# A two-layer hybrid trunk on one core: first loads, GLA state sums, RWKV state products, attention transposes and the last norm rearranged

## The chip, the core and the metric

The kernel runs on one core of one Trainium2 chip. The metric is the device time of one execution in microseconds; all times below are microseconds unless ns is said. TensorE (PE) multiplies matrices out of SBUF into PSUM, VectorE (DVE), ScalarE (ACT) and GpSimd (POOL) work on vectors, and SyncE (SP) issues most DMAs. Each of them runs its own instructions in a fixed order, so an instruction that waits holds up all that is behind it on its engine.

## What is computed

`x` is 512 tokens of 1024 features, in fp32. Each of two layers mixes tokens, attends to a memory of 256 tokens and applies a gated feed-forward net; a norm ends the trunk. The first layer's mixer is GLA beside RWKV-7, the second's is RG-LRU beside mLSTM. Cut to what the change touches:

```python
mem_n = rms_norm(mem, mem_norm_g)
h = x
for layer in range(2):
    xn = rms_norm(h, norm_mix_g[layer])
    proj = xn @ w_in
    if layer == 0:                               # y_b: mLSTM in layer 1
        y_a, y_b = gla_group(proj[..., :GLA_COLS]), rwkv7_group(proj[..., GLA_COLS:])
    h = h + concat([y_a, y_b]) @ w_mix_out[layer]
    h = h + memory_cross_attention(rms_norm(h, g), mem_n)  # 4 heads of 256, softmax over 256
    h = h + conv_glu_ffn(rms_norm(h, g))
return rms_norm(h, final_norm_g)

# gla_chunked: 8 chunks of 64 tokens, 4 heads
scores = where(causal, q_dec @ k_inv.T, 0);  o_local = scores @ v
o_state = q_c @ S;  S = S * sd_c + ke_c.T @ v_c

# rwkv7_chunked: 8 heads of 64
z_state, z_local = triangular_solve(I - A_ab, [a_dec, A_ak @ v])
z = zs @ S.T + zl                                # one step a chunk
y = rd @ S.T + arb @ z + yl
S = S * sd + z.T @ be + v_c.T @ ke_c
```

## The kernel before

Features lie on the 128 partitions, tokens along the free axis, so an activation is eight tiles of 128x512 (four for a half). Each fp32 factor is split into two fp32r parts, and a product is three matmuls (hi·hi, hi·lo, lo·hi). `wload` brings in a weight tile of 128x1024 (512 KB): a DMA on SP's queue into `raw` (ring `wr`, three buffers), a copy to `wh` on ACT, and a subtraction to `wl` on DVE, which frees the `raw` buffer. `dense` then issues 24 matmuls of 128x512 that sum into one PSUM tile of the pool `mm` (three buffers); these are the "dense matmuls" below, mm<-xs,wh and mm<-xs,wl in the profile. Small products go to the PSUM pool `ax` (five buffers). `qr` is a ring of sixteen 128x512 tiles named `xs`. The function `mmul` is line 209, `act` line 206, `tt` 194, `stt` 203, so most rows name these lines and are told apart by tiles.

What order the instructions of each engine take is settled when the program is built: a scheduler takes the program's operations with their dependences and places one list on each engine. `issue_after` makes an operation wait in that list for a given instruction. Nothing is reordered when the program runs.

**Head.** Set-up loads vectors (`vec`) and constants (`cmat`: identity, a block matrix `bo64`, the mask `rmask`), runs warm-up matmuls on a constant tile, and scales `bo64` to `bo64m` on DVE. `trunk` then loads x's first tile, a small weight (`walr`, made on ACT and DVE from its own load), the GLA key weights `wk`, and x's other seven tiles.

**GLA** (line 593): after the projections, scores are masked into `sc` by copies on DVE; `kt` and `v` give the state sums (28 products for two head pairs and seven chunks), `S` is updated by chunk on DVE, and both feed the outputs.

**RWKV** (line 767) treats p = 0..3, two heads each. Per p: three dense blocks r, k, v (72 dense matmuls), `wa,w2a` products for decay and gate, a chain of exponentials on ACT (`e1`, `a`), a scan on DVE (`e2`, line 814), norm of k (`kn,cmat`), the stacks `stk`, `bk`, products `stk,bk` masked into `bb` and `stk`, transposes into SV and BKT, and a bonus product `xs,cmat`. After p=0 `during` calls `memory_norm` (line 484): it loads the memory in four tiles, squares them on ACT and adds them into `nacc` on DVE; the rest of it runs after p=2. Then comes a triangular solve, mostly on DVE, beside the memory's key projections, and the chunk loop: eight chunks, each with products stk,sv (w), sv,stk (yp), ws,bb (z), sv,bkt (uu) and bb,sv (yp), eight of each kind, with the memory's projections as dense matmuls of 128x256 among them.

**Attention** (`heads`, line 427): per head and half, scores, softmax parts `mx`, `e`, `sm`, then four transposes of `e` into `pT`. **End** (`finish`, line 1336): for each half of the tokens, the last add to h, the norm's sum, and eight products h * gain * r with four stores.

Of the kernel before, what the change touches and what calls it, by code (L numbers as in the profile page):

```python
# [20 lines left out]
KD = 8  # L21
# [121 lines left out]
class Trunk:  # L143
    def __init__(self, ctx, tc, I):
# [14 lines left out]
        nc.gpsimd.dma_start(out=self.cm, in_=I["cmat"][:, 0:384])  # L159
# [10 lines left out]
        for i in range(10):  # L170
            self.mmul(warm[:, 0:P], self.ones["d"], self.ones["d"])
# [6 lines left out]
        nc.vector.tensor_scalar(out=self.bo64m, in0=self.bo64, scalar1=1.0 / 64.0, scalar2=None, op0=ALU.mult)  # L178
# [61 lines left out]
    def wload(self, src, kb, m):  # L240
# [4 lines left out]
        n = kb * m  # L245
        self.last_load = nc.sync.dma_start(out=raw[:, :n], in_=src.rearrange("p k m -> p (k m)"))
        self.act(hi[:, :n], raw[:, :n], AF.Copy)
        self.tt(lo[:, :n], raw[:, :n], hi[:, :n].bitcast(F32), ALU.subtract)
        sh = lambda t: t[:, :n].rearrange("p (k m) -> p k m", m=m)
# [149 lines left out]
def xattn(K, l, nm, kd, vd, h, feed):  # L399
    nc, X = K.nc, nm.X  # L400
    with ExitStack() as es:
# [25 lines left out]
        def heads(hd, q):  # L427
            pT = [K.ax.tile([P, T], F32, name="ax") for _ in range(2)]
            for half in range(2):
# [18 lines left out]
                for i in range(2):  # L448
# [3 lines left out]
                    for m in range(2):  # L452
                        nc.tensor.transpose(pT[m][:, t * P:(t + 1) * P], e[:, i, m * P:(m + 1) * P], K.ident)  # L453
# [30 lines left out]
def memory_norm(K, sm):  # L484
# [5 lines left out]
    for i in range(4):  # L490
# [3 lines left out]
        sq = K.qr.tile([P, T], F32, name="xs") if i else acc  # L494
# [7 lines left out]
    r = K.qr.tile([P, T], F32, name="xs")[:, 0:256]  # L502
# [90 lines left out]
def gla(K, nm, wga, wk, squares, after, Y):  # L593
    nc, X = K.nc, nm.X
    with ExitStack() as es:
# [5 lines left out]
        with K.tc.issue_after(after.ins):  # L601
            nc.vector.tensor_copy(out=gm, in_=gf)
        wa = gp.tile([48, 256], F32, name="walpha")
# [96 lines left out]
        for p in range(2):  # L700
            us = {}
            for c in range(7):
                if c % 4 < 2:
                    us[c // 4, c % 2] = K.ax.tile([P, 2, P], F32, name="ax")
                u = us[c // 4, c % 2][:, (c % 4) // 2]
                r = slice(64 * (c % 2), 64 * (c % 2) + 64)
                for e in range(2):
                    hd = 2 * p + e
                    K.mmul(u[64 * e:64 * e + 64], kt[p][r, c // 2, 64 * e:64 * e + 64],
                           v[r, c // 2, hd * P:(hd + 1) * P])  # L710
                if c == 0:
# [55 lines left out]
def rwkv(K, X, Y, during, after):  # L767
# [3 lines left out]
    with ExitStack() as core:  # L771
# [12 lines left out]
        with ExitStack() as es:  # L784
# [13 lines left out]
            vp = wt.tile([P, 640], F32, name="vp")  # L798
            nc.gpsimd.memset(vp, 0.0)
            for p in range(4):  # L800
                r = shifted(K, new(), K.block("w_rw", p, X), p, om)
                k = shifted(K, new(), K.block("w_rw", 4 + p, X), 4 + p, om)
                v = shifted(K, vp[:, 64:576], K.block("w_rw", 8 + p, X), 8 + p, om)
# [28 lines left out]
                for w0, w1 in ((0, 4), (4, 8), (8, 9)):  # L832
                    ps = K.ax.tile([P, 4, P], F32, name="ax")
                    for w in range(w0, w1):
                        nc.tensor.transpose(ps[:, w - w0], vp[:, w * 64:w * 64 + P], K.ident)
# [532 lines left out]
```

## Time and profile before

| | us |
|---|---|
| median of 3 runs | 1558.81 (1558.35 to 1563.36) |
| profiled execution | 1558.83 |
| its span | 1557.0 |
| PE busy | 1527.6 |
| DVE busy | 914.9 |
| ACT busy | 683.7 |
| POOL busy | 23.3 |

The span runs from the first to the last instruction of the profiled execution; 1.8 lie around it. The page gives shares for the whole span, so a stage has to be read from the rows of its own stretch. A matmul is pipelined: its mean in a list of groups is its latency, and what it costs in a stream is the spacing, best seen in the chain of waits, which gives the time of a whole run of them. The mean granted clock of PE is 0.996 of 2.4 GHz; a few stretches lie under that.

### The profile page before, as it was taken

Reading aid. Unit: us, or ns where it says so; the run is one execution under the profiler, and the core shown is the slowest. Engines: PE = TensorE matmul, PEld = TensorE weight load, DVE = VectorE, ACT = ScalarE, POOL = GpSimd, SP = SyncE. Lnnn points to the kernel's source line nnn. Section 1 sums busy time; section 2 is a strip of 40 time slices with the busy share of each in tenths; the row PEclk is TensorE's granted clock in tenths of the full one; section 3 lists DMA queues with packets and bytes.
Section 4 is the critical chain, followed back from the end, with each engine's and each line's share of the span. In section 5 each row is a group of like instructions: output and inputs, shape, how many; then the busy total and the mean of one; then the engine's idle time right before and its main releaser. Section 6 shows DMA issues by size and latency. Waiting matters only on the chain.

```text
span 1557.0 us, 20187 instructions
## 1 busy us (share of the span) xinstructions
PE 1527.6 (98%) x8077; PEld 1240.3 (80%) x8077; DVE 914.9 (59%) x1348; ACT 683.7 (44%) x1101; POOL 23.3 (1%) x62
## 2 busy tenths in 40 slices
PE   8999999999999999999999999999999999999997
PEld 6876777787888888888888878788888888888886
DVE  7537679645655755556633386777557556565333
ACT  5465563345444543333332267566345333333221
POOL 2000000001000000000000000000000000000000
PEclk9999999999999999999999999999999999999999
DMA  4222226226331333332233321224213333322332
GB/s 165 81 75 82 68 62 192 90 93 224 111 106 48 107 97 98 99 95 95 92 98 102 94 98 49 75 73 149 72 51 117 105 98 95 96 95 89 101 98 78
DMA packets 50175, 152.19 MB, mean 98 GB/s; under 512 B 5505, under 2 KB 8865, under 8 KB 50081
## 3 DMA queue, kind: packets, MB, share of 16 engines
q1 hardware_dynamic: 45664, 142.87, 29.2%
q10 hardware_dynamic: 3536, 5.38, 1.0%
q0 software_dynamic: 880, 2.66, 0.4%
q8 instruction: 63, 1.03, 0.3%
q14 instruction: 32, 0.25, 0.1%
HBM read 144.59 MB, written 6.29 MB: 97 GB/s over the span
## 4 chain that ended last, share of the span: by engine, by line
PE 89%; DVE 6%; ACT 3%; DMA 1%; issue 1%; SPq 0%; DVEq 0%; ACTq 0%
PE mm L209 77%; PE ax L209 10%; DVE wl L194 1%; ACT e L206 1%; PE ax L453 1%; ACT wh L206 1%; DVE tm L194 1%; DVE bb L892 0%; DVE tu L194 0%; DMA raw<-in_w_kv 0%; DMA raw<-in_w_gla 0%; DVE au L881 0%; DVE e L814 0%; ACT a L206 0%; DVE stk L203 0%
## 5 line engine op out<-in xcount | busy, mean ns | idle before, releaser
L209 PE MATMUL mm<-xs,wh 128*128 128x512 f32 (+1 forms) x3627 | 1110.4, 387 | 2.4 <-DVE vp L203 1.8
L209 PEld LDWEIGHTS mm<-xs,wh 128*128 128x128 f32 x3627 | 671.8, 188 | 147.9 <-issue 8.0
L209 PE MATMUL mm<-xs,wl 128*128 128x512 f32 (+1 forms) x1814 | 700.3, 386 | 0.6 <-DVE wl L194 0.5
L206 ACT ACTIVATE wh<-raw 128x1024 fp32r<-128x1024 f32 (+2 forms) x273 | 264.8, 970 | 528.5 <-PE mm L209 412.1
L194 DVE TENSOR_TENSOR wl<-raw,wh 128x1024 fp32r<-128x1024 f32 (+2 forms) x272 | 302.6, 1113 | 211.8 <-ACT wh L206 210.8
L209 PEld LDWEIGHTS mm<-xs,wl 128*128 128x128 f32 x1814 | 341.0, 188 | 71.9 <-issue 1.8
L194 DVE TENSOR_TENSOR upad<-mm,rstd 128x512 f32<-128x512 f32 (+1 forms) x52 | 35.9, 690 | 95.5 <-PE mm L209 95.3
L194 DVE TENSOR_TENSOR h<-h,mm 128x512 f32<-128x512 f32 (+1 forms) x73 | 49.5, 677 | 69.3 <-PE mm L209 69.1
L194 DVE TENSOR_TENSOR g<-mm,rstd 128x512 f32<-128x512 f32 (+1 forms) x44 | 30.4, 692 | 76.0 <-PE mm L209 75.9
L203 DVE SCALAR_TENSOR_TENSOR c<-upad,vec,c 128x512 f32<-128x512 f32 (+1 forms) x88 | 65.9, 749 | 3.3 <-ACT c L206 1.8
L209 PE MATMUL mm<-wh,xs 128*128 128x256 f32 (+1 forms) x256 | 66.4, 349 | 0.0
L206 ACT ACTIVATE c<-c 128x512 f32<-128x512 f32 (+1 forms) x44 | 27.8, 632 | 87.1 <-DVE c L203 87.1
L209 PEld LDWEIGHTS mm<-wh,xs 128*128 128x128 f32 x256 | 44.8, 194 | 6.3 <-issue 1.0
L209 PE MATMUL mm<-wl,xs 128*128 128x256 f32 (+1 forms) x128 | 45.3, 354 | 3.8 <-DVE wl L194 3.8
L206 ACT ACTIVATE xs<-g 128x512 fp32r<-128x512 f32 (+1 forms) x44 | 27.8, 633 | 26.9 <-DVE g L194 26.9
L206 ACT ACTIVATE c<-upad,vec 128x512 f32<-128x512 f32 (+1 forms) x44 | 35.3, 802 | 1.5 <-DVE upad L194 1.5
L206 ACT ACTIVATE e<-ax,mx,scl 128x256 f32<-128x256 f32 x32 | 17.8, 560 | 39.8 <-DVE mx L194 39.8
L194 DVE TENSOR_TENSOR g<-c,g 128x512 f32<-128x512 f32 (+1 forms) x44 | 30.4, 692 | 5.8 <-ACT c L206 1.4
L194 DVE TENSOR_TENSOR nacc<-nacc,nsq 128x512 f32<-128x512 f32 x45 | 32.8, 730 | 0.3
L203 DVE SCALAR_TENSOR_TENSOR xs<-h,vec,xs 128x512 fp32r<-128x512 f32 x40 | 29.9, 749 | 3.5 <-ACT xs L206 3.4
L194 DVE TENSOR_TENSOR xs<-ax,xs 128x512 fp32r<-128x512 f32 x32 | 21.3, 687 | 18.0 <-ACT xs L206 18.0
L206 ACT ACTIVATE xs<-h,vec 128x512 fp32r<-128x512 f32 x40 | 28.8, 719 | 6.5 <-DVE h L194 6.5
(353 smaller groups left out, 1221.9 us busy)
## 6 DMA issues: line engine op xcount, KB each, us to landing
raw<-in_w_up SPq DMA_DIRECT2D x86, 512.0 KB, 3.4
raw<-in_w_dn SPq DMA_DIRECT2D x32, 512.0 KB, 3.4
raw<-in_w_kk SPq DMA_DIRECT2D x16, 512.0 KB, 3.6
raw<-in_w_kv SPq DMA_DIRECT2D x16, 512.0 KB, 3.9
raw<-in_w_q SPq DMA_DIRECT2D x16, 512.0 KB, 3.6
raw<-in_w_o SPq DMA_DIRECT2D x32, 256.0 KB, 2.6
raw<-in_w_cd SPq DMA_DIRECT2D x16, 512.0 KB, 3.2
raw<-in_w_rw SPq DMA_DIRECT2D x14, 512.0 KB, 3.6
```

Source lines behind the costliest of these rows:

```text
L194: (eng or self.nc.vector).tensor_tensor(out=out, in0=a, in1=b, op=op)
L203: return self.nc.vector.scalar_tensor_tensor(out=out, in0=a, scalar=s, in1=b, op0=op0, op1=op1)
L206: return self.nc.scalar.activation(out=out, in_=a, func=f, **kw)
L209: self.last_mm = self.nc.tensor.matmul(out, lhsT=l, rhs=r, start=start, stop=stop)
L453: nc.tensor.transpose(pT[m][:, t * P:(t + 1) * P], e[:, i, m * P:(m + 1) * P], K.ident)
```

## The change

Seven parts:

- **First loads.** `cmat` is loaded on SP behind x, not on POOL; `wk` comes in two halves, each followed by a tile of x, with the copy and subtraction per half; 16 warm-up matmuls instead of 10; `bo64m` is made inside GLA.
- **memory_norm.** The three squares, and later the tile for the norm's factor, are taken from the ring `raw` instead of `qr`.
- **GLA state sums.** Two PSUM tiles of a whole bank hold the seven sums of a pair; all fourteen products are issued before the updates of S.
- **RWKV values.** v lies in a plain tile; four transposes and four copies per p instead of nine and five.
- **RWKV chunk loop.** `group` holds seven of eight products behind the first, with e=1 before e=0.
- **Attention.** The transposes of both halves follow the second half's softmax.
- **End.** The last norm's gain is multiplied into seven of the eight tiles on ACT when they are fed to the norm; `finish` multiplies blocks of three tiles by r and stores three pieces a half.

```diff
@@ class Trunk, set-up @@
         self.cm = con.tile([P, 384], F32, name="cmat")
-        nc.gpsimd.dma_start(out=self.cm, in_=I["cmat"][:, 0:384])
...
-        for i in range(10):
+        for i in range(16):
             self.mmul(warm[:, 0:P], self.ones["d"], self.ones["d"])
...
-        nc.vector.tensor_scalar(out=self.bo64m, in0=self.bo64, scalar1=1.0 / 64.0, scalar2=None, op0=ALU.mult)
@@ wload @@
-    def wload(self, src, kb, m):
+    def wload(self, src, kb, m, parts=1, between=None):
...
-        n = kb * m
-        self.last_load = nc.sync.dma_start(out=raw[:, :n], in_=src.rearrange("p k m -> p (k m)"))
-        self.act(hi[:, :n], raw[:, :n], AF.Copy)
-        self.tt(lo[:, :n], raw[:, :n], hi[:, :n].bitcast(F32), ALU.subtract)
-        sh = lambda t: t[:, :n].rearrange("p (k m) -> p k m", m=m)
+        n = kb * m // parts
+        src = src.rearrange("p k m -> p (k m)")
+        for i in range(parts):
+            s = slice(i * n, (i + 1) * n)
+            self.last_load = nc.sync.dma_start(out=raw[:, s], in_=src[:, s])
+            if between:
+                between(i)
+        for i in range(parts):
+            s = slice(i * n, (i + 1) * n)
+            self.act(hi[:, s], raw[:, s], AF.Copy)
+            self.tt(lo[:, s], raw[:, s], hi[:, s].bitcast(F32), ALU.subtract)
+        sh = lambda t: t[:, :kb * m].rearrange("p (k m) -> p k m", m=m)
@@ xattn, heads @@
-            pT = [K.ax.tile([P, T], F32, name="ax") for _ in range(2)]
+            es = []
             for half in range(2):
...
-                    for m in range(2):
-                        nc.tensor.transpose(pT[m][:, t * P:(t + 1) * P], e[:, i, m * P:(m + 1) * P], K.ident)
+                    es.append(e[:, i])
+            pT = [K.ax.tile([P, T], F32, name="ax") for _ in range(2)]
+            for m in range(2):
+                for t in range(4):
+                    nc.tensor.transpose(pT[m][:, t * P:(t + 1) * P], es[t][:, m * P:(m + 1) * P], K.ident)
@@ memory_norm @@
-        sq = K.qr.tile([P, T], F32, name="xs") if i else acc
+        sq = K.wr.tile([P, 1024], F32, name="raw")[:, :T] if i else acc
         K.act(sq, f, AF.Square)
         if i:
             K.add(acc, acc, sq)
...
-    r = K.qr.tile([P, T], F32, name="xs")[:, 0:256]
+    r = K.wr.tile([P, 1024], F32, name="raw")[:, 0:256]
@@ gla @@
             nc.vector.tensor_copy(out=gm, in_=gf)
+            nc.vector.tensor_scalar(out=K.bo64m, in0=K.bo64, scalar1=1.0 / 64.0, scalar2=None, op0=ALU.mult)
...
         for p in range(2):
-            us = {}
+            us = [K.ax.tile([P, 4, P], F32, name="ax") for _ in range(2)]
             for c in range(7):
-                if c % 4 < 2:
-                    us[c // 4, c % 2] = K.ax.tile([P, 2, P], F32, name="ax")
-                u = us[c // 4, c % 2][:, (c % 4) // 2]
+                u = us[c % 2][:, c // 2]
                 r = slice(64 * (c % 2), 64 * (c % 2) + 64)
                 for e in range(2):
                     hd = 2 * p + e
                     K.mmul(u[64 * e:64 * e + 64], kt[p][r, c // 2, 64 * e:64 * e + 64],
                            v[r, c // 2, hd * P:(hd + 1) * P])
+            for c in range(7):
+                u = us[c % 2][:, c // 2]
                 if c == 0:
                     K.act(S[:, p, 0], u, AF.Copy)
                 else:
@@ rwkv, loop over p @@
-            vp = wt.tile([P, 640], F32, name="vp")
-            nc.gpsimd.memset(vp, 0.0)
...
-                v = shifted(K, vp[:, 64:576], K.block("w_rw", 8 + p, X), 8 + p, om)
+                v = shifted(K, new(), K.block("w_rw", 8 + p, X), 8 + p, om)
...
-                for w0, w1 in ((0, 4), (4, 8), (8, 9)):
-                    ps = K.ax.tile([P, 4, P], F32, name="ax")
-                    for w in range(w0, w1):
-                        nc.tensor.transpose(ps[:, w - w0], vp[:, w * 64:w * 64 + P], K.ident)
-                    if w0 < 8:
-                        K.act(SV[0][64:128, w0:w1, p], ps[64:128, :, 0:64], AF.Copy)
-                    w = max(w0, 1)
-                    K.act(SV[1][0:64, w - 1:w1 - 1, p], ps[0:64, w - w0:w1 - w0, 64:128], AF.Copy)
+                ps = K.ax.tile([P, 4, P], F32, name="ax")
+                for t in range(4):
+                    nc.tensor.transpose(ps[:, t], v[:, t * P:(t + 1) * P], K.ident)
+                for e in range(2):
+                    for i in range(2):
+                        K.act(SV[e][R[1 - e], i::2, p], ps[R[i], :, R[e]], AF.Copy)
@@ rwkv, chunk loop @@
+            def group(products):
+
+                products[0]()
+                with K.tc.issue_after(K.last_mm.ins):
+                    for f in products[1:]:
+                        f()
+
...
-                for p in range(4):
-                    for e in range(2):
-                        K.mmul(w[R[e], p], stk[e][:, p, c, 0:64], SV[e][:, c, p])
+                group([lambda e=e, p=p: K.mmul(w[R[e], p], stk[e][:, p, c, 0:64], SV[e][:, c, p])
+                       for p in range(4) for e in (1, 0)])
...
-                    for p in range(4):
-                        for e in range(2):
-                            K.mmul(uu[R[e], p], BKT[:, p, c, R[e]], SV[e][:, c, p])
+                    group([lambda e=e, p=p: K.mmul(uu[R[e], p], BKT[:, p, c, R[e]], SV[e][:, c, p])
+                           for p in range(4) for e in (1, 0)])
...
-                for p in range(4):
-                    for e in range(2):
-                        K.mmul(yp[R[e], p], SV[e][R[e], c, p], BB[R[e], p, c, 64:128], False, p == 3)
+                group([lambda e=e, p=p: K.mmul(yp[R[e], p], SV[e][R[e], c, p], BB[R[e], p, c, 64:128], False, p == 3)
+                       for p in range(4) for e in (1, 0)])
@@ trunk, start @@
-            wk = K.wload(I["w_gla"][:, 2], KD, P)
-            for k in range(1, KD):
+            rest = iter(range(1, KD))
+            wk = K.wload(I["w_gla"][:, 2], KD, P, 2, lambda i: load(next(rest)))
+            for k in rest:
                 load(k)
+            nc.sync.dma_start(out=K.cm, in_=I["cmat"][:, 0:384])
@@ trunk, end @@
-                    for j in range(KD):
-                        K.stt(h[j][:, s], h[j][:, s], K.v("final_norm_g", j), r, ALU.mult, ALU.mult)
-                        if j % 2:
-                            (nc.sync, nc.scalar)[j // 2 % 2].dma_start(out=dst[:, j - 1:j + 1, s],
-                                                                      in_=ht[:, j - 1:j + 1, s])
-
-                ffn(K, l, nf, h, nm.feed, finish)
+                    rb = r.rearrange("p (o m) -> p o m", o=1)
+                    for a, b in ((0, 3), (3, 6), (6, 8)):
+                        c = min(b, KD - 1)
+                        K.mul(ht[:, a:c, s], ht[:, a:c, s], rb.to_broadcast([P, c - a, 256]))
+                        if b > c:
+                            K.stt(h[c][:, s], h[c][:, s], K.v("final_norm_g", c), r, ALU.mult, ALU.mult)
+                        (nc.scalar if a == 3 else nc.sync).dma_start(out=dst[:, a:b, s], in_=ht[:, a:b, s])
+
+                def feed(j, t):
+
+                    nm.feed(j, t)
+                    K.act(t, t, AF.Copy, scale=K.v("final_norm_g", j))
+
+                ffn(K, l, nf, h, feed, finish)
```

What this moves on the engines, at three places.

SP, from the last weights of p=0 (raw_1042) over p=1's three weight tiles (raw_1210, raw_1244, raw_1277), before:

```order
L246 DMA raw_1042<-in_w_rw 128x1024 [waits DMAHW3_49,DVE_49]
L792 DMA w2a2_894<-in_w_w2a2 128x512 [waits DMASW1_49,DVE_49,PE_49]
L246 DMA raw_1210<-in_w_rw 128x1024 [waits DMAHW4_49,DVE_49]
L246 DMA raw_1244<-in_w_rw 128x1024 [waits DMAHW5_49,DVE_49]
L246 DMA raw_1277<-in_w_rw 128x1024 [waits DMAHW6_49,DVE_49]
L246 DMA raw_1425<-in_w_gla 128x1024 [waits DMAHW0_49,DVE_49]
```

The three tiles follow w2a2; the memory's tiles xs come behind them and behind more weights. The same place after (p=1's tiles are raw_1206, raw_1240, raw_1274):

```order
L248 DMA raw_1046<-in_w_rw 128x1024 [waits DMAHW5_49,DVE_49]
L802 DMA w2a2_899<-in_w_w2a2 128x512 [waits DMASW0_49,DVE_49,PE_49]
L501 DMA xs_1187<-in_memT 128x2x256
L501 DMA xs_1190<-in_memT 128x2x256
L501 DMA xs_1195<-in_memT 128x2x256
L501 DMA xs_1200<-in_memT 128x2x256
L248 DMA raw_1206<-in_w_rw 128x1024 [waits DMAHW6_49,DVE_49]
L248 DMA raw_1240<-in_w_rw 128x1024 [waits DMAHW7_49,DVE_49]
L248 DMA raw_1274<-in_w_rw 128x1024 [waits DMAHW0_49,DVE_49]
```

The memory's four tiles now stand ahead of p=1's weights, and the three buffers that p=1's tiles wait for are those of the squares. DVE after, from p=0's last instruction (xs_1184, the bonus) on; e2_1316 is p=1's scan, raw_1192 to raw_1202 are the squares, wl_1208 to wl_1276 belong to p=1's weights:

```order
L192 TENSOR_TENSOR xs_1184<-ax_1182,xs_1045 128x512
L822 SCALAR_TENSOR_TENSOR e2_1316<-reset65_974,e1_1311 128x520
L192 TENSOR_TENSOR nacc_1186<-nacc_1186,raw_1192 128x512
L192 TENSOR_TENSOR nacc_1186<-nacc_1186,raw_1197 128x512
L192 TENSOR_TENSOR nacc_1186<-nacc_1186,raw_1202 128x512
L192 TENSOR_TENSOR wl_1208<-raw_1206,wh_1207 128x1024
L192 TENSOR_TENSOR wl_1242<-raw_1240,wh_1241 128x1024
L192 TENSOR_TENSOR wl_1276<-raw_1274,wh_1275 128x1024
```

The adds that give the buffers back stand behind p=0 and p=1's scan; before, wl of p=1's tiles stood among p=0's steps and the squares lay in other tiles.

PE at the start of p=0, before (wa,w2a opens p; vp is v in its padded tile):

```order
L209 MATMUL ax<-wa,w2a_894 128x512 x2
L209 MATMUL ax<-kn,cmat 128x512
L209 MATMUL mm<-xs,wh 128x512 x2
L835 MATMUL ax<-cmat,vp 128x128 x9
L209 MATMUL mm<-xs,wl 128x512
```

Dense matmuls of p=1 follow at once and go on between the small products: 31 ahead of the first stk,bk, 9 among the stk,bk, 32 behind the bonus, and then p=1's own wa,w2a. PE at the same place, after:

```order
L207 MATMUL ax<-wa,w2a_899 128x512 x2
L207 MATMUL ax<-kn,cmat 128x512
L842 MATMUL ax<-cmat,xs 128x128 x4
L207 MATMUL ax<-stk_880,bk 64x128
L207 MATMUL ax<-stk_881,bk 64x128
```

No dense matmul stands there, nor between the 64 stk,bk products that follow; p=0's end after reads:

```order
L865 MATMUL ax<-cmat,bk 128x128 x4
L207 MATMUL ax<-xs,cmat 128x512
L207 MATMUL ax<-wa,w2a_899 128x512 x2
L207 MATMUL mm<-xs,wh 128x512 x2
L207 MATMUL mm<-xs,wl 128x512
```

The bonus xs,cmat is followed by p=1's wa,w2a, and only then by p=1's 72 dense matmuls.

PE in the chunk loop before, from the matmuls behind ws,bb to the second product of the group sv,bkt (numbers tell the two halves e of SV):

```order
L209 MATMUL mm<-xs,wl 128x256
L209 MATMUL mm<-xs,wh 128x256
L209 MATMUL ax<-sv_879,bkt 64x64
L209 MATMUL ax<-bb,sv_879 64x64
L209 MATMUL mm<-xs,wh 128x256
L209 MATMUL mm<-xs,wl 128x256
L209 MATMUL mm<-xs,wh 128x256 x2
L209 MATMUL mm<-xs,wl 128x256
L209 MATMUL mm<-xs,wh 128x256 x2
L209 MATMUL mm<-xs,wl 128x256
L209 MATMUL ax<-sv_880,bkt 64x64
L209 MATMUL ax<-sv_879,bkt 64x64
```

The first product of sv,bkt and of bb,sv stands alone, eight dense matmuls ahead of the other seven. The same place after:

```order
L207 MATMUL mm<-xs,wl 128x256
L207 MATMUL mm<-xs,wh 128x256 x2
L207 MATMUL ax<-sv_885,bkt 64x64
L207 MATMUL ax<-sv_884,bkt 64x64
L207 MATMUL ax<-sv_885,bkt 64x64
L207 MATMUL ax<-sv_884,bkt 64x64
L207 MATMUL ax<-sv_885,bkt 64x64
L207 MATMUL ax<-sv_884,bkt 64x64
L207 MATMUL ax<-sv_885,bkt 64x64
L207 MATMUL ax<-sv_884,bkt 64x64
L207 MATMUL ax<-bb,sv_885 64x64
L207 MATMUL ax<-bb,sv_884 64x64
```

The eight products of each kind stand together, behind one run of dense matmuls.

## Rows read from the trace of the kernel before

**Rows 1.** Busy time, share of the span and instructions, from the page

```profile
PE 1527.6 (98%) x8077; PEld 1240.3 (80%) x8077; DVE 914.9 (59%) x1348; ACT 683.7 (44%) x1101; POOL 23.3 (1%) x62
```

**Rows 2.** PE's waits over the span: who waited for what: us, times, longest

```profile
PE mm L209 <- DVE wl L194: 4.3, 3, 3.3
PE ax L209 <- DVE bk L194: 3.6, 4, 1.5
...
PE ax L209 <- DVE sc L698: 0.8, 2, 0.6
PE mm L209 <- ACT wh L206: 0.6, 1, 0.6
...
PE ax L835 <- DVE vp L203: 0.5, 2, 0.3
```

**Rows 3.** Windows: us, busy PE PEld DVE ACT POOL, PEclk, DMA share, GB/s

```profile
2.00:7.00 5.00, 4.64 (x20) 4.34 (x20) 0.00 (x0) 1.60 (x3) 4.66 (x19) 1.00 0.97 300
10.70:14.20 3.50, 3.10 (x7) 1.80 (x8) 3.50 (x6) 3.50 (x7) 0.00 (x0) 0.51 1.04 419
256.00:262.00 6.00, 6.00 (x21) 4.79 (x20) 5.71 (x12) 1.06 (x1) 0.00 (x0) 0.72 0.78 262
```

**Rows 4.** Timeline, four places of PE: start us, us, what [idle before <-releaser]

```profile
8.29 0.40 PE L209 MATMUL mm<-xs,walr 128*48 128x512 f32 x1 [1.43 <-DVE walr L194]
...
111.35 1.13 PE L209 MATMUL ax<-wa,w2a 64*128 64x512 f32 x4
...
140.44 0.50 PE L209 MATMUL mm<-xs,wh 128*128 128x512 f32 x1 [1.78 <-DVE vp L203]
...
230.20 1.02 PE L209 MATMUL ax<-xs,cmat 128*128 128x512 f32 x2
```

**Rows 5.** Chain of waits, the head: start us, us, what

```profile
8.73 1.07 ACT wh L206
...
9.82 1.24 DVE wl L194
...
11.10 12.65 PE mm L209 x48
```

**Rows 6.** Chain of waits, within GLA's state sums

```profile
69.83 0.43 PE mm L209
```

**Rows 7.** Chain of waits, p=0

```profile
128.85 0.59 PE ax L859 x4
...
130.30 7.08 PE mm L209 x31
```

**Rows 8.** Chain of waits, p=3

```profile
213.87 1.11 PE ax L209 x4
...
217.60 1.25 DVE e L814
...
224.98 1.09 PE ax L209 x16
```

**Rows 9.** DMA issues of p=1's weights, 90 to 106: KB each, us to landing

```profile
raw<-in_w_rw SPq DMA_DIRECT2D x3, 512.0 KB, 3.6
```

**Rows 10.** Adds of squares, from the page's groups: busy us, mean ns

```profile
L194 DVE TENSOR_TENSOR nacc<-nacc,nsq 128x512 f32<-128x512 f32 x45 | 32.8, 730 | 0.3
```

**Rows 11.** Chain of waits, one chunk of the RWKV loop

```profile
310.97 0.38 PE ax L209 x4
311.34 0.31 PE mm L209
311.66 1.08 PE ax L209 x28
...
313.78 0.78 PE mm L209 x5
314.56 0.51 PE ax L209 x4
```

**Rows 12.** Timeline, the end on DVE

```profile
1550.36 3.25 DVE L203 SCALAR_TENSOR_TENSOR h<-h,vec,nsq 128x256 f32<-128x256 f32 x8 [2.19 <-ACT nsq L206]
```

## The prediction, made before the changed kernel ran

> **What bounds the kernel now.** The page's first section comes first: TensorE (PE) is busy 98% of the span [rows 1]. So a change pays where it removes PE work or one of PE's waits, and costs where it makes PE wait. I then read PE's waits over the whole span [rows 2]: together they are a few per cent, in single places. Last come the stretches that the diff touches, in order of time, by the chain of waits and the timeline: the head [rows 3 to 5], GLA's state sums [rows 6], the first RWKV slice p=0 [rows 4, 7], the last one p=3 [rows 4, 8], the RWKV chunk loop [rows 11] and the end [rows 12].
>
> The sum is made on the profiled execution: span 1557.0, reported 1558.8, which is the median of the runs shown (1558.81). All times are microseconds. Under 0.3% (4.7) a measurement of this kernel can't be told from no change.
>
> **Head.** Before, the first real matmul starts at 8.29 and has waited 1.43 for walr [rows 4], whose subtraction stands on VectorE (DVE) behind bo64m and so behind a constant load; then PE waits 0.6 for wh and about 1.0 for wl (4.3 less the single 3.3, which lies much later) [rows 2], because the 512 KB weight tile is copied in 1.07 and subtracted in 1.24 as a whole [rows 5]. From 10.7 to 14.2 the granted clock is 0.51, so 3.5 x 0.49 = 1.7 are lost [rows 3]. After, bo64m is gone from there, the weights come in halves, and 16 warm-up matmuls stand where 10 did. Ten took at most 4.64 [rows 3], so six more take up to 2.8, of which 1.43 was waited anyway: the first real matmul starts up to 1.4 later; I take 1.0. Gain: 0.6 + 1.0 + 1.7 - 1.0 = 2.3, as long as the halves land before 9. If they land late and the clock falls again, it is 0; if all the waits go and nothing starts later, 3.3. I take **-2.3** (0 to -3.3).
>
> **GLA state sums.** The 28 products of the state sums stood in pieces with a single 128x512 matmul between: 0.43 for such a matmul [rows 6] against 0.228 in a stream (7.08 for 31) [rows 7], three times, so 0.6; and PE waits 0.8 in two places for sc [rows 2], which the products can cover when all stand together. With the pieces' own switches I take **-1.5** (0 to -2.2): the S updates now start later, and nothing else covers those.
>
> **RWKV, p=0: the loss.** Before, p=1's three weight tiles were loaded during p=0: their DMAs waited only for older subtractions, and 72 matmuls of p=1 fill PE between p=0's small products and behind them. After, memory_norm's squares occupy all three buffers of `raw`; the loads of p=1's weights wait for the three adds nacc<-nacc,raw, and those stand on DVE behind all of p=0 and behind p=1's first scan. SyncE's queue issues in order, so every later load is behind these as well, and PE has not one dense matmul between p=0's first and last product.
>
> Count from T, p=0's first wa matmul (111.35 before [rows 4]). The nearest row is p=3 before, whose products run nearly without dense matmuls between: wa at 213.87, scan at 217.60 (+3.7), first stk products at 224.98 (+11.1) [rows 8], last product (xs,cmat) at 230.20 (+16.3) [rows 4]. After, p=1's wa comes right behind that, at T+17.2; its scan 3.7 later, T+20.9; the scan takes 1.25 [rows 8] and the first add 0.73 [rows 10]: T+22.9. The load needs 3.6 to land [rows 9], the copy wh 1.07 [rows 5]: T+27.6, when two matmuls run; wl another 1.24 [rows 5]: T+28.8. The remaining 70 matmuls at 0.228 end at T+44.8. Before, the same 72 and p=1's wa are done when PE goes on at 140.44 [rows 4], T+29.1. That is 15.7. Four dense matmuls (some 1.0) stand inside p=3's chain and none in p=0's now, so 14.7. PE has then been nearly idle for some 10; before, behind its wait of 3.3 for wl [rows 2], the next 6 were granted 0.72, a loss of 1.7 [rows 3]. I take **+16.5**. From below: DVE has three subtractions of 1.24 fewer among p=0's steps than before, and the chain could end 4 earlier, +12. From above: 22, by the first rival's mechanism.
>
> **RWKV, p=1 to 3.** Five transposes fewer in each: four take 0.59 in the chain [rows 7], 15 of them 2.2 at most; nearer 1.7 in a run. PE's waits for bk (3.6 in four places) and for vp (0.5) [rows 2] shrink for p=1 and p=3, whose wa and gates now run a slice ahead: 1.4. **-3.1** (-1 to -5). The four copies into SV instead of five on ScalarE (ACT) and the missing fill of vp on POOL lie beside PE's work: nothing; uncovered, each is under the wh copy's 1.07 [rows 5].
>
> **Triangular solve.** PE waits 3.3 for wl there [rows 2]: DVE is the bound, and one subtraction (1.24) fewer stands among its steps, but as much of PE's work is deferred. **-0.3** (-2 to +1).
>
> **RWKV chunk loop.** Here PE has no idle time and loses by switching. One chunk of 7.6 reads: a product pair 0.38, one matmul 0.31, the rest of that group 1.08, and later five matmuls 0.78, a pair 0.51 [rows 11]. One matmul 0.31 against five 0.78 makes 0.12 for each and 0.19 for each separate stretch. In a run, 28 passes take 1.08, so a pair's four would be 0.15. A group split after its first product thus costs 0.38 - 0.15 + 0.19 = 0.42 (sv,stk) or 0.51 - 0.15 + 0.19 = 0.55 (sv,bkt). The change closes seven of the second kind, five of the first and a smaller one at the end: 3.85 + 2.1 + 0.3: **-6.2** (-2 to -8). The lower end holds if the copies that feed the groups aren't ready earlier: before, 5 + 8 matmuls stand between ws,bb and the second product, after 14, which are quicker by some 0.6 with the stretch and the pair gone.
>
> **Attention.** As many transposes, one run of eight a head, with a dozen matmuls ahead of it in two heads and seven or eight in the other two. No row shows PE's array waiting for e. If four heads came to wait as sc is waited for, 0.4 each [rows 2], it would be +1.6, and as much could be saved: **0** (-1.6 to +1.6).
>
> **End.** Eight scaled products take 3.25 on DVE [rows 12]; three block products and one scaled one do the same elements with four starts fewer. I take one of the eight pieces, 0.4: **-0.4** (-1.6, four pieces, to +0.4 if the larger first store holds up the last). The gain's seven ACT operations lie ahead of the last matmuls, beside PE's work.
>
> **Sum.** -2.3 - 1.5 + 16.5 - 3.1 - 0.3 - 6.2 + 0 - 0.4 = +2.7: **1561.5**.
>
> **Rivals.**
> *The clock stays low through p=0 (slower).* For: the granted clock falls behind stretches where PE waits [rows 3], and after the change PE has over 25 of those on end. Then p=0's own products run at half speed too. In p=3 sixteen passes take 1.09 [rows 8], and p=0 has 64 such and eight transposes, some 5 in all, of which about 4 stand in the chain; with the restart itself slow for longer, another 2: the loss is 22.5. From +2 beyond my term the sum passes 0.3%. Against: much of these products' time is start-up, not columns. Time: 1567.5.
> The Trainium skill, "TensorE: Matmul & The Clock Gate", section "HAM oscillation — how this bites in real kernels", says that a matmul kernel which waits for data between bursts starts each burst at the lower clock again. Rows 3 agree (0.72 behind the gap). By that rule alone only the restart is priced, as in my term; the sum stays 1561.5.
> *The chunk loop is bound by its dependences.* Then the waits of the split products move to the head of the groups, and of 6.2 only 2 are left: 1565.7. For: 0.6 less cover per chunk. Against: no wait for sv stands among PE's waits of before.
> *The stall is shorter and the gains whole (faster).* p=0's steps alone on DVE and ACT end 4 earlier, the head gives 3.3, the loop 8, p=1 to 3 give 4: 12.5 - 3.3 - 8 - 4 - 1.5 - 0.7 = -5.0: 1553.8. For: three subtractions fewer stand among p=0's steps. Against: p=3 before has few of those either, and still needs 16.3.
> *The loads are not held.* If p=1's weights came early anyhow, only the gains would be left, -13.8: 1545. Against: the order names the waits, and nothing else could let a buffer go; 2 in 100.
>
> **How the numbers follow.** My forecast, its terms some 4 off either way in sum: 0.52, of which 0.36 within 0.3%, 0.12 above, 0.04 below. The low clock 0.23 (slower). The bound loop 0.10: half within 0.3%, half above. The shorter stall 0.13: 0.10 faster, 0.03 within. The loads not held 0.02: faster. Faster 0.16, same 0.44, slower 0.40. For 8 in 10 the range takes in the first and the third, and most of the second and fourth: 1554 to 1569.
>
> **What would show it.** p=0: from the first wa to the end of the 72 matmuls some 45 instead of 29, PE waiting 8 or more for p=1's wh and wl, and a granted clock under 0.8 in the stretch behind; no load of w_rw issued between p=0's wa and the scan. Loop: chunks of 6.5 to 6.8 for the same number of dense matmuls, and no wait for sv; waits for sv or z would mean the third case. Head: no clock of 0.51 behind 10.7, and the 48 matmuls that start at 11.10 before [rows 5] done 2.3 earlier. End: DVE's last work 2.8 long. I am wrong if the RWKV weights are issued before the adds, if p=0 takes under 40, or if the loop's chunks stay above 7.2.

## The result, and the profile after

The changed kernel takes 1571.36 us in the median of four runs (1568.74 to 1574.62) where the kernel before takes 1558.58 (four runs, one more than in the table above): a ratio of 1.0077 (95% interval 1.0049 to 1.0105). It is slower by 12.8; forecast were 2.7 and a range that ended at 1569. The span of the profiled execution is 1569.6 against 1557.0, so it has the difference in it: 12.6.

The page of the changed kernel, first section, and PE's waits over the span, which answer to [rows 1, 2]:

```profile
PE 1522.0 (97%) x8069; PEld 1238.0 (79%) x8069; DVE 914.3 (58%) x1341; ACT 689.8 (44%) x1105; POOL 22.6 (1%) x60
```

```profile
PE mm L207 <- ACT wh L204: 13.6, 3, 9.3
PE ax L207 <- issue: 10.4, 3, 8.5
PE mm L207 <- DVE wl L192: 4.2, 4, 2.4
...
PE ax L207 <- DVE bk L192: 1.1, 3, 0.6
```

PE has less work than before and still ends later. Two waits for weights are new (9.3 in one place, 4.0 in another, both for the copy wh), and so is one of 8.5 for which the profile names no releaser ("issue"). That one lies inside p=0, ahead of its first stk,bk, where no dense matmuls stand any more to cover the steps on ACT and DVE. What was to shrink did: bk 3.6 to 1.1.

Where the 12.6 arise, by PE's own instructions that exist in both kernels (start in the timeline; between two marks the same work is done except where the last column says):

| from, to | before | after | difference | work moved past the mark |
|---|---|---|---|---|
| start, p=0's first wa | 111.35 | 107.53 | -3.8 | |
| p=2's first wa | 175.82 | 190.31 | +18.3 | |
| p=3's bonus product | 230.20 | 246.49 | +1.8 | 10 passes of 128x256 later |
| first ws,bb of the loop | 282.92 | 299.23 | 0.0 | those 10 here; 14 dense 128x512 later |
| last ws,bb of the loop | 335.92 | 345.20 | -7.0 | those 14 here; 23 dense 128x256 later |
| layer 0's ones_d,nacc behind its FFN's start | 435.04 | 447.42 | +3.1 | those 23 here |
| end of the span | 1557.0 | 1569.6 | +0.2 | |

Three of the seven parts pay about as forecast: the first loads and GLA's sums 3.8 together before p=0, the loop 7. Between p=0 and p=3 all of it is lost and more. PE's wait inside p=0, and the chain of waits of the changed kernel through p=0 and the stretch behind (start, us, what):

```profile
118.67 1.51 PE L207 MATMUL ax<-stk,bk 64*64 64x128 f32 x10 [8.52 <-issue]
```

```profile
107.60 1.11 PE ax L207 x4
...
120.35 1.97 PE ax L207 x21
...
123.36 1.92 PE ax L207 x32
...
125.87 1.97 PE ax L207 x6
...
130.50 1.24 DVE e L822
131.74 0.59 DVE nacc L192
...
132.35 3.61 DMA raw<-in_w_rw
...
135.99 1.06 ACT wh L204
...
138.35 17.98 PE mm L207 x70
```

This is the chain that the prediction counted, in its order: p=0's small products, p=1's wa, scan, add, load, copy, subtraction, 70 matmuls. And by windows (us, busy PE, PEld, DVE, ACT, POOL, PEclk, DMA share, GB/s):

```profile
107.50:126.00 18.50, 9.82 (x84) 6.83 (x84) 11.66 (x16) 10.24 (x21) 0.11 (x1) 0.72 0.00 1
126.00:137.00 11.00, 1.79 (x6) 0.30 (x4) 5.20 (x8) 9.14 (x17) 0.00 (x0) 0.77 0.27 81
137.00:143.00 6.00, 5.87 (x14) 4.21 (x15) 2.45 (x2) 1.10 (x2) 0.00 (x0) 0.56 0.67 213
143.00:156.20 13.20, 13.20 (x60) 10.92 (x59) 5.15 (x6) 4.05 (x6) 0.00 (x0) 1.00 0.37 114
```

```profile
118.60:125.20 6.60, 6.36 (x68) 5.04 (x68) 4.11 (x6) 1.29 (x4) 0.00 (x0) 0.50 0.01 2
125.20:126.60 1.40, 1.40 (x10) 0.69 (x6) 1.24 (x2) 0.68 (x2) 0.00 (x0) 1.00 0.00 0
```

From 107.5 to 126 the DMA engines move 1 GB/s: nothing is being loaded. The granted clock is 0.50 (1.2 GHz) in the 6.6 in which p=0's products start, behind the 8.5 of idle time, and 1.00 from 125.2 on; behind the second wait it is 0.56 over six.

The second stall stands ahead of p=3's 72 dense matmuls. PE's timeline:

```profile
211.20 1.13 PE L207 MATMUL ax<-wa,w2a 64*128 64x512 f32 x4
216.35 0.72 PE L207 MATMUL mm<-xs,wh 128*128 128x512 f32 x2 [4.02 <-ACT wh L204]
217.75 0.80 PE L207 MATMUL mm<-xs,wl 128*128 128x512 f32 x1 [0.68 <-DVE wl L192]
```

and what SP, ACT and DVE do for p=3's weights:

```profile
187.09 29.86 SPq L248 DMA_DIRECT2D raw<-in_w_rw  x3
...
212.57 0.40 ACT L204 ACTIVATE raw<-raw 128x256 f32<-128x256 f32 x1
...
213.31 3.25 DVE L201 SCALAR_TENSOR_TENSOR xs<-xs,vec,raw 128x256 f32<-128x256 f32 x8
...
215.24 1.05 ACT L204 ACTIVATE wh<-raw 128x1024 fp32r<-128x1024 f32 x1
...
216.63 0.33 SPq L248 DMA_DIRECT2D raw<-in_w_rw  x1
```

The tile `raw` that the eight products read is memory_norm's factor r, the other tile that the change put into the weight ring. Of p=3's three loads the first two went out by 192.5, and nothing was loaded between 196 and 216; the third goes out when r's eight readers end, at 216.6. But PE does not wait for the third here. It waits for the copy wh of the first, whose weights have been there for over 20: ACT makes it at 215.24, without a pause before it, because its list has r's two steps and p=3's exponentials first.

The head, a window that answers to [rows 3], and the chunk loop's chain, that answers to [rows 11]:

```profile
10.70:14.20 3.50, 3.50 (x17) 2.31 (x16) 3.50 (x6) 3.50 (x7) 0.00 (x0) 1.00 1.04 400
```

```profile
327.94 1.30 PE ax L207 x32
...
334.58 1.29 PE ax L207 x32
335.88 1.26 PE mm L207 x9
...
337.17 1.15 PE ax L207 x32
...
338.63 0.61 PE ax L207 x16
```

The clock no longer falls at 10.7. In the loop a chunk is 6.64 long (327.94 to 334.58 in the chain) instead of 7.6 for the same 24 dense matmuls and 80 small passes, and the products stand in runs of 32 and 16 passes.

### The profile page after: what moved, and what is told of

Same layout as the page of the kernel before. It is cut to its first block, busy times and chain, and to the rows that moved or that the text cites. A ratio compares the mean times of both kernels' runs of the same rounds, so it can differ in the third digit from the quotient of the medians.

```text
span 1569.6 us, 20153 instructions
## 1 busy us (share of the span) xinstructions
PE 1522.0 (97%) x8069; PEld 1238.0 (79%) x8069; DVE 914.3 (58%) x1341; ACT 689.8 (44%) x1105; POOL 22.6 (1%) x60
## 4 chain that ended last, share of the span: by engine, by line
PE 86%; DVE 7%; ACT 3%; issue 2%; DMA 1%; SPq 0%; POOL 0%; DVEq 0%; ACTq 0%
PE mm L207 75%; PE ax L207 10%; DVE wl L192 1%; ACT wh L204 1%; DVE tu L192 1%; DVE tm L192 1%; PE ax L462 1%; ACT e L204 1%; DMA raw<-in_w_kv 0%; ACT xs L204 0%; DMA x<-in_xT 0%; DVE au L887 0%; DVE xs L192 0%; PE ax L865 0%; DVE stk L201 0%
## 5 line engine op out<-in xcount | busy, mean ns | idle before, releaser
L207 PE MATMUL mm<-xs,wh 128*128 128x512 f32 (+1 forms) x3627 | 1109.3, 387 | 13.4 <-ACT wh L204 13.3
L207 PEld LDWEIGHTS mm<-xs,wh 128*128 128x128 f32 x3627 | 674.2, 188 | 158.8 <-ACT wh L204 16.4
L207 PE MATMUL mm<-xs,wl 128*128 128x512 f32 (+1 forms) x1814 | 703.1, 388 | 0.8 <-DVE wl L192 0.7
L207 PEld LDWEIGHTS mm<-xs,wl 128*128 128x128 f32 x1814 | 342.1, 189 | 72.4 <-DVE wl L192 2.8
L207 PE MATMUL mm<-wh,xs 128*128 128x256 f32 (+1 forms) x256 | 65.9, 347 | 0.3 <-ACT wh L204 0.3
L207 PEld LDWEIGHTS mm<-wh,xs 128*128 128x128 f32 x256 | 44.2, 192 | 6.3 <-ACT kt L204 0.8
L207 PE MATMUL mm<-wl,xs 128*128 128x256 f32 (+1 forms) x128 | 44.8, 350 | 3.5 <-DVE wl L192 3.5
L192 DVE TENSOR_TENSOR xs<-ax,xs 128x512 fp32r<-128x512 f32 (+1 forms) x36 | 24.0, 686 | 20.8 <-ACT xs L204 20.8
L192 DVE TENSOR_TENSOR xs<-g,xs 128x512 fp32r<-128x512 f32 (+1 forms) x44 | 30.1, 685 | 2.5 <-ACT xs L204 2.5
```

Of the source, the lines that this page charges most:

```text
L192: (eng or self.nc.vector).tensor_tensor(out=out, in0=a, in1=b, op=op)
L207: self.last_mm = self.nc.tensor.matmul(out, lhsT=l, rhs=r, start=start, stop=stop)
```

## The experiments

Theory M: the loss comes from memory_norm's tiles in the weight ring, from the squares at p=0 and from r at p=3, each by itself. Rivals: the second stall follows from the first; or the loss needs the plain v tile of RWKV as well (Q below). Each of the first four runs undoes or does one piece. Times are medians; the ratio is to the kernel before, which ran beside them at 1559.4 to 1559.7. The changed kernel was measured beside 1558.6, so a difference to it is good to about 1.

**Squares and factor back in the xs ring.**

```diff
-        sq = K.wr.tile([P, 1024], F32, name="raw")[:, :T] if i else acc
+        sq = K.qr.tile([P, T], F32, name="xs") if i else acc
-    r = K.wr.tile([P, 1024], F32, name="raw")[:, 0:256]
+    r = K.qr.tile([P, T], F32, name="xs")[:, 0:256]
```

> The changed kernel with memory_norm as before: the squares and the factor tile in the ring of sixteen xs tiles. Theory M (all of the loss comes from memory_norm's tiles in the weight ring): p=0 has its dense matmuls back (the order shows 41 ahead of and 31 behind its small products), PE waits under 2 in the slices p=0 to 3 instead of about 15, from p=0's first wa to the end of p=1's 72 matmuls 28 to 30 instead of 48.7, the wait of 4 at p=3 gone: 1571 - 19 - 5 = 1546 to 1549. Rival Q (the plain v tile needs the sixteen tiles, so the squares would wait for those instead): a stall stays in p=0 or p=1, 1555 or more.

1553.02, ratio 0.9950 (0.9929 to 0.9971): 18.3 less than the changed kernel, and faster than the kernel before. M holds for the loss as a whole. But 1546 to 1549 was expected, and one wait of PE, 1.8 at the same place before [rows 4], is long:

```profile
138.27 0.80 PE L207 MATMUL mm<-xs,wh 128*128 128x512 f32 x1 [5.92 <-DVE xs L201]
```

So a part of rival Q is there too: something makes p=1 wait 5.9. Its chain of waits runs through the memory's loads and adds:

```profile
126.73 1.24 DVE wl L192
...
127.98 0.34 SPq L248
...
128.37 4.78 DMA xs<-in_memT
...
136.86 0.69 DVE nacc L192
137.55 0.67 DVE xs L201
```

The third and fourth memory tile are loaded only at 128, because SP has a weight load ahead of them that waits for wl; DVE waits for their squares with p=1's evictions queued behind, and PE waits for those.

**Only the squares back.** The first of the two edits alone.

> The changed kernel with only the three squares back in the xs ring; the factor tile r stays in the weight ring. Theory M: the stall at p=0 goes (about -19), the one at p=3 (4 of waiting for wh, then the low clock) stays: 1552 to 1554. If the p=3 wait was a consequence of p=0's, it goes too: 1547.

1558.80, ratio 0.9991 (0.9974 to 1.0008): 12.6 less than the changed kernel, where 1552 to 1554 was expected. The wait for wh at p=3 is still there, 4.0. So it isn't a consequence of p=0's. The wait ahead of p=1 is there as well (5.8); with it 12.6 come to 18.4, near the 19 expected.

**Only the factor back.** The second alone.

> The changed kernel with only the factor tile r back in the xs ring; the squares stay in the weight ring. Theory M: p=0 as in the changed kernel (48.7 from its first wa to the end of the 72 matmuls), no wait for wh at p=3: 1564 to 1567. If the p=3 wait was p=0's consequence: 1571.

1566.03, ratio 1.0041 (1.0025 to 1.0057): 5.3 less than the changed kernel, as expected. p=0 keeps its stall (PE waits 9.5 for wh there) and p=3 has none. ACT's first copy of p=3's weights stands 17 earlier than in the changed kernel:

```profile
197.97 1.05 ACT L204 ACTIVATE wh<-raw 128x1024 fp32r<-128x1024 f32 x1
```

The two pieces, 12.6 and 5.3, add up to 17.9, about what both together gave (18.3): two independent causes. That r's place makes the stall at p=3 is shown by these runs; why the scheduler then lists the copies behind r's steps was not tried.

**memory_norm alone changed, on the kernel before.** The two edits reversed, nothing else.

> The kernel before with memory_norm alone changed (squares and factor tile in the weight ring). Theory M: both stalls appear without any other part of the change, +18 to +20 at p=0 and +4 to +7 at p=3: 1581 to 1585. Rival Q (the loss needs the plain v tile in the xs ring): under 1565.

1588.45, ratio 1.0193 (1.0161 to 1.0224). Both stalls appear without any other part: PE waits 9.6 for wh ahead of p=1's 72 matmuls and 4.0 ahead of p=3's. Q falls. The loss is larger than the 1581 to 1585 expected, 29 in the median and 25.1 in the profiled spans (1582.1 against 1557.0). 17.3 of it lie between p=0's first wa and p=2's (110.74 to 192.51), much as in the changed kernel (18.3); the rest is spread over p=2 and 3 and the stretch behind the loop, where work has moved past the marks, and wasn't taken apart.

**The products of the loop alone in groups.** `group` and its three uses, on the kernel before.

> The kernel before with group() in the RWKV chunk loop alone. Theory G (the split products cost PE's switching, as worked out in the prediction): 6 to 7.5 less, 1551 to 1553, chunks of 6.6 to 6.9 instead of 7.6, no wait for sv in the loop. Rival (the loop is bound by its dependences): -2, 1556.5, with waits for sv or z.

1555.28, ratio 0.9978 (0.9958 to 0.9998); the profiled span is 5.2 shorter. From the first to the last ws,bb it takes 47.0 instead of 53.0, and PE waits for sv 0.3 in one place. From the chain of one chunk to the next:

```profile
313.15 1.30 PE ax L209 x32
314.45 1.26 PE mm L209 x9
...
315.73 1.15 PE ax L209 x32
...
319.80 1.30 PE ax L209 x32
```

6.65 a chunk (313.15 to 319.80), as in the changed kernel. Theory G holds in the loop's trace; the timed gain, 0.3 to 6.5 by its interval, lies under the 6 to 7.5 expected in its middle (4.4). The rival of the loop bound by its dependences falls.

**Constant matmuls in the gap at p=1: does the clock cost what was put down?**

```diff
                 K.mmul(psa, w2a2[64:128, p * P:(p + 1) * P], wa[64:128])
+                if p == 1:
+                    with K.tc.issue_after(K.last_mm.ins):
+                        warm = K.ax.tile([P, T], F32, name="ax")
+                        for i in range(14):
+                            K.mmul(warm[:, 0:P], K.ones["d"], K.ones["d"])
```

> The changed kernel with 14 matmuls of constants put on PE between p=1's wa products and its 72 dense matmuls, where PE waits for weights; the rest of the order is the same. Theory C (the 72 matmuls run slow only because PE's granted clock is down when they start): they take 16.4 instead of 18.4 to 19.1, the granted clock of their stretch is 0.95 or more instead of 0.86, and the kernel is 1.5 to 2.5 faster, 1569. Rival (they are slow because weights arrive late): no change in their time, 1571 or, if the constants delay the start, 1572.

1571.13: no change. The size was wrong: the 28 passes lasted 3.4, PE then stood idle for 6.3 more, and the clock fell again (0.61 from 136 to 142):

```profile
126.44 3.39 PE L207 MATMUL ax<-ones_d 128*128 128x128 f32 x28
136.11 1.22 PE L207 MATMUL mm<-xs,wh 128*128 128x512 f32 x2 [6.27 <-ACT wh L204]
```

That run decides nothing between theory and rival, so 36 were tried.

> As the run with 14 constant matmuls, with 36: there 28 passes took 3.4, so that PE stood idle for 6.3 after them and the clock fell again (0.61 in the 6 behind). 36 last some 8.7, to about the moment at which p=1's first weights are ready. Theory C: the granted clock in the 6 behind is 0.95 or more instead of 0.56, the 72 matmuls take 16.4 to 17.6 (two of them, and the wait for wl, stay), 1.5 to 2 less than in the changed kernel: 1569 to 1570. Rival (late weights): 19 as before, 1571.

Now the gap is filled to 1.4, and the window behind it is

```profile
136.00:142.00 6.00, 5.47 (x24) 4.43 (x24) 1.83 (x2) 1.30 (x2) 0.00 (x0) 1.00 0.74 231
```

with the chain's `136.66 16.17 PE mm L207 x70` where it was 17.98. Theory C holds: 1.8 of the 72 matmuls' time was the low clock. The kernel as a whole gains 0.9 in the median (1570.50, ratio 1.0065, 1.0041 to 1.0089), which can't be told from none; 1569 to 1570 was expected.

**The plain v tile alone, on the kernel before.**

```diff
-                v = shifted(K, vp[:, 64:576], K.block("w_rw", 8 + p, X), 8 + p, om)
+                v = shifted(K, new(), K.block("w_rw", 8 + p, X), 8 + p, om)
```

with the four transposes of the change.

> The kernel before with the plain v tile and four transposes alone, memory_norm as before. The order of its slices is that of the changed kernel with the norm's tiles back in the xs ring. Theory V (v in the xs ring takes a place that memory's tiles had, so these are loaded late and p=1 waits 5.9): +2 to +5 for that wait, less 1.7 for twenty transposes fewer and less some 2 of waits: 1557 to 1561. Rival (the saving stands alone, the wait has another cause): 1554 to 1556.

1562.85, ratio 1.0021 (0.9997 to 1.0044): no gain; 3 more in the median, where 1557 to 1561 was expected, and an interval that takes in none. PE waits 5.6 for an eviction ahead of p=1, where it waited 1.8 before [rows 4]. That wait, then SP's issues of the memory's tiles up to there, in the kernel before (two lines) and in this run (two lines):

```profile
PE mm L209 <- DVE xs L203: 5.6, 1, 5.6
```

```profile
124.33 1.45 SPq L492 DMA_DIRECT2D xs<-in_memT  x3
134.68 0.43 SPq L492 DMA_DIRECT2D xs<-in_memT  x1
```

```profile
124.22 0.94 SPq L492 DMA_DIRECT2D xs<-in_memT  x2
134.08 0.95 SPq L492 DMA_DIRECT2D xs<-in_memT  x2
```

So far this agrees with theory V: with v in the ring of sixteen xs tiles, the third of the memory's tiles, which come out of the same ring, is loaded 9 later.

**v in a tile of its own**, on the first experiment's kernel:

```diff
-                v = shifted(K, new(), K.block("w_rw", 8 + p, X), 8 + p, om)
+                v = shifted(K, wt.tile([P, T], F32, name="v"), K.block("w_rw", 8 + p, X), 8 + p, om)
```

> The changed kernel with memory_norm's tiles in the xs ring and the plain v in a tile of its own instead of that ring. Theory V (the plain v takes a place of the xs ring, for which the memory's loads wait): the 5.9 that PE waited ahead of p=1 shrinks to under 2.5, 1547 to 1549. Rival (the wait comes from the order on SyncE and VectorE alone): 1552 to 1553.

1549.11, ratio 0.9924 (0.9900 to 0.9949): 3.9 less than with v in the ring, and the 5.9 have become 2.6, now for v; both lie just outside what was expected. That v's place in the ring costs time is shown. The way that theory V gives for it is not: the memory's last two tiles are loaded at 128.0, as with v in the ring (128.4). What differs is the order of evictions on DVE. With v in the ring, and then with v in its own tile:

```profile
136.86 0.69 DVE L192 TENSOR_TENSOR nacc<-nacc,xs 128x512 f32<-128x512 f32 x1 [2.33 <-ACT xs L204]
137.47 2.06 DVE L201 SCALAR_TENSOR_TENSOR xs<-mm,vec,xs 128x511 f32<-128x511 f32 x3
```

```profile
133.67 0.74 DVE L201 SCALAR_TENSOR_TENSOR v<-mm,vec,v 128x511 f32<-128x511 f32 x1
135.95 0.69 DVE L192 TENSOR_TENSOR nacc<-nacc,xs 128x512 f32<-128x512 f32 x1 [1.54 <-ACT xs L204]
```

All three of p=1's evictions stood behind the last add of memory_norm; v's own now stands ahead of it, and PE goes on behind that.

**memory_norm called behind p=1 instead of behind p=0**, on the first experiment's kernel:

```diff
-            if p == 0:
+            if p == 1:
                 M.append(memory_norm(K, sm))
                 next(M[0])
-            elif p == 1:
                 gla_gate(K, X, Y, 0)
```

> The changed kernel with memory_norm's squares and factor in the xs ring and its call moved from behind p=0 to behind p=1. Theory M2 (with the squares in the xs ring the 5.9 that PE waits ahead of p=1 come from the memory tiles, whose loads stand on SyncE's queue behind weights, and whose adds stand on VectorE ahead of p=1's evictions): the wait ahead of p=1 goes, 4 to 6 less than with the call behind p=0, 1547 to 1549. Rival (the wait comes back one slice later, ahead of p=2): 1552 to 1554.

1547.67, ratio 0.9930 (0.9915 to 0.9945): the fastest version here, 11 less than the kernel before and 24 less than the changed one. Yet the theory behind it holds only in part: the wait came back one slice later, as the rival said (PE waits 5.5 for an eviction ahead of p=2), and the time fell all the same. Layer 0's ones_d,nacc stands at 423.2 instead of 429.2, and the mean granted clock is 0.995 instead of 0.992, which is 0.3% of the span, 4.6; the difference in clock lies between 107 and 300, where PE also stands idle in places and a low clock costs nothing. So how much of the 5.4 is clock is a reading, not a test.

**Both reliefs together.**

> As the run before, with memory_norm called behind p=1 too. If both causes add up: 1542 to 1545, PE waits under 2.5 ahead of p=2. If one relief suffices: 1547 to 1548, as with the late call alone.

1549.53, ratio 0.9936 (0.9911 to 0.9960). Neither 1542 to 1545 nor 1547 to 1548 came: the reliefs don't add up, and PE waits 5.7 ahead of p=2 here too, with v out of the ring. In both runs with the late call the evictions behind memory_norm's last add are those of GLA's gates (xs<-xs,vec,mm at 161.7 here, 161.9 in the run before), which v's tile doesn't touch.

**The first loads alone**, on the kernel before (set-up, `wload` in halves, 16 warm-up matmuls, `bo64m` in GLA).

> The kernel before with the first loads alone (constants on SyncE behind x, weights in halves, 16 warm-up matmuls, bo64m in GLA). By the changed kernel's trace the first RWKV slice starts 3.8 earlier with GLA's part in it, and the second walpha product 1.7 earlier: 1.5 to 2.5 less, 1556.5 to 1557.5. Rival: nothing is left at the end, 1559.

1558.26, ratio 0.9997 (0.9979 to 1.0014): not told from none in time; the profiled span is 2.2 shorter, and p=0's first wa stands at 108.79 instead of 111.35. That is 2.6 at p=0, near the 2.3 of the prediction; the median, with 1556.5 to 1557.5 expected, doesn't show it at the end.

GLA's sums, the attention and the end were not run alone.

## Why the prediction was wrong, point by point

| term | forecast | by the marks above |
|---|---|---|
| head and GLA | -3.8 | -3.8 |
| p=0's stall | +16.5 | +19.6 |
| p=1 to 3 | -3.1 | +2.7 (p=1 -1.3, p=2 and 3 +4.0) |
| triangular solve | -0.3 | +1.0 |
| chunk loop | -6.2 | -7.5 |
| attention and end | -0.4 | +0.6 |
| sum | +2.7 | +12.6 |

(The work moved past marks is counted at 0.216 for a pass of the ten, 0.227 for a 128x512 and 0.12 for a 128x256. p=0's stall is the time from its first wa to the end of p=1's 72 matmuls, 107.53 to 156.18, less the 29.1 of before.)

**The step that failed: p=1 to 3, forecast at -3.1, measured at +2.7.** memory_norm's factor r was put at nothing, without a reason. The prediction saw that p=3's wa had moved ahead of its 72 dense matmuls and counted that as a gain, "whose wa and gates now run a slice ahead". It was part of a second stall: with r in the weight ring, p=3's copies wh stand behind r's steps on ACT, and the third load waits for r's eight readers on DVE. Only the three squares were followed to what waits behind them. The run with r alone put back gives 5.3 for it; without these 5.3 the term would be -2.6. The edit to r stands in the diff just under that of the squares; with 5.3 for it the sum would have been +8.0, 1567. That is still under the measured 1571.36, so this step is the largest part of the miss of 10 and not the whole of it.

**A term that was mis-sized: p=0, by 3.1.** The mechanism was right in every link. The first stk products start at T+11.1 as in p=3 [rows 8]. From there to the bonus the forecast had 4.2 (p=3's 5.2, less 1.0 for its dense matmuls), and it took 7.0 (118.67 to 125.70), because the granted clock was 0.50 until 125.2: 32 passes took 1.92 there and 1.10 in p=3 before:

```profile
228.74 1.10 PE ax L209 x32
```

This is the first rival's mechanism at 2.8, where it had 4 for these products and 2 more for the restart. The argument against it, that much of their time is start-up, was wrong: their time nearly doubled. The price stayed lower because the clock came back before the products ended. From p=1's wa on the links were 3.8 to the scan's start, 1.24, 0.6, 3.61, 1.06: as read from before. The restart's 1.7 was measured at 1.8.

**A term that is right partly by luck: head and GLA.** Up to the first qd,ki product (65.19 before, 63.36 after) the head gave 1.8 of its 2.3; the first real matmul started 1.5 earlier (8.29, 6.83) and not 1.0 later, and new waits of 0.9 twice came behind it. GLA's sums then gave the rest, 2.0 instead of 1.5, both inside their ranges.

**What else was off.** For the triangular solve 1.0 was lost where 0.3 of gain was forecast; the cause was not looked for. In the loop the fixed price for each separate stretch [rows 11] was right within a fifth: -7.5 against -6.2. Attention and the end: 0.6 lost from the loop's end on, 0.2 of it behind layer 0's mark, where 0.4 of gain was forecast. DVE's last products take 2.16 and 0.48, 2.6 instead of 3.25 [rows 12], but the span ends 3.8 behind the last of them instead of 3.4: the stores need 2.6 or more to land, before 2.2.

**A term that hid another.** The transposes and waits of p=1 to 3 were costed as if the plain v tile were free. Alone it brings no gain that can be measured, though transposes are saved, and with memory_norm's tiles in the xs ring v's place there costs 3.9. In the changed kernel that price doesn't show: its longest wait for an eviction into xs is 0.9, in the head. So the stall of p=0 costs the changed kernel 19.6 in the trace, but undoing it alone gives back 12.6.

Of the chances, 0.40 lay on slower and 0.44 on no change. The signs named for p=0 and the loop came: 48.7 for p=0, loads behind the adds, PE waiting 9.3, a clock under 0.8; and chunks of 6.6, with 0.3 of waits for sv in the whole loop where none was forecast.

## What to carry to other kernels

A ring of buffers that feeds the bottleneck's weights must not lend a buffer to a tile whose last reader stands late in another engine's order: each tile lent is a hold on a load, and each has to be followed, from its last reader to the first matmul that the load feeds. The copies of weights that have landed have to be looked up in the new order too: at p=3 the longest wait was for one of those. When an order shows an operation running earlier than before, ask first whether the work that stood ahead of it was held up. And an edit that saves work by taking a tile from a shared ring is to be priced with the ring: here a tile of its own for v was worth 3.9.

## What the runs showed of the hardware

The granted clock at the start of the record isn't to be trusted: the window from 2 to 7 shows 1.00 [rows 3], but its 128x128 passes are spaced 0.23 (20 in 4.64), while 28 of the same passes took 3.39 in the gap at p=1, 0.12 each. By that the head's warm-up ran at 1.2 GHz, and matmuls of constants cost half as much elsewhere; the run with 14 was too short for that reason.

Idle PE costs twice here: between p=0 and p=1 it waits for data, and of the 72 matmuls behind it 70 take 17.98, or 16.17 when the gap is filled with matmuls of constants. The same holds inside p=0: behind 8.5 of idle time the granted clock was 0.50 for 6.6, although the products then followed each other with one pause of 0.17.
